# The MLP's squares on ScalarE, and another order of the three matmuls of a split product

## The chip, the cores and the metric

The kernel runs on one core of one Trainium2 chip. The time is the device time of one execution in microseconds. The kernel before was run three times: median 1261.39 us, from 1261.08 to 1261.54.

## The reference

A decoder trunk of two layers on 512 tokens with 1024 features, all in fp32. Layer 0 has a forgetting attention with 16 heads, layer 1 a gated short convolution; each is followed by an MLP and by a gated embedding. What the change touches is the MLP, and every product of a weight with activations:

```python
def sq_relu_mlp(h, w_up, w_down):
    return jnp.square(jax.nn.relu(h @ w_up)) @ w_down

for i in range(DEPTH):                       # DEPTH = 2
    ...                                      # attention (i = 0) or convolution (i = 1)
    f = sq_relu_mlp(rmsnorm(x, g[2]), w_mlp_up[i], w_mlp_down[i])
    x = x + rmsnorm(f, g[3])
    gate = jax.nn.sigmoid(rmsnorm(x, g[4]) @ w_ple_gate[i])
    e = (p[i] @ w_ple_proj[i]) * gate
    x = x + rmsnorm(e, g[5])
```

`w_mlp_up` is 1024 x 4096, `w_mlp_down` 4096 x 1024.

## The kernel before

**Split products.** A fp32 operand is kept as a pair: a high part rounded to the matmul's format (fp32r) and the low part that is left. `split` (line 230) makes it: ScalarE casts the high part, another engine subtracts it from the source for the low part (VectorE for plain weights and activations, GpSimd for weights that were combined first). `mm3` (line 222) multiplies two pairs by three matmuls into one bank of PSUM: high by high (line 224), and the two products of a low part with a high part (lines 225 and 226). Its first argument is the stationary operand, its second the moving one. There are two kinds of callers. Where `narrow` gives the weights, they are the first argument: up in the MLP, q and k, the convolution's input. Where `wide` gives them, they are the second argument and the activations the first: down in the MLP, v, the outputs of the mixers, the gated embedding. The program has 1784 such products. Names in the profile: `wh`, `wl` are a weight's parts, `hTh`, `hTl` those of the normalised and transposed tokens, `raw` a weight as loaded.

**The MLP** (`mlp`, line 704) goes over 8 groups of 512 hidden features. In a group, `up` (line 710) makes four blocks of 128 hidden features for all 512 tokens, 8 products each over the 1024 inputs (24 matmuls; in group 0 the tokens are taken in two halves of 256). ScalarE reads the bank with a relu into `r` (line 722), and `square` (line 707) makes `q = r * r`. For groups 0 to 6 `down` (line 750) multiplies by 7 products in place of 8 (a Strassen scheme over halves of the hidden features, tokens and outputs): `quarters` and `halves` make sums of quarters of `q` on GpSimd (`s`) and split them (`A11`, `A12`, `A22`, `S1` to `S4`, with h and l for the parts; the pair A12, A22 is one tile named A12, S1 and S2 one named S1, S3 and S4 one named S3); the combined weights `T1` to `T4` are made on GpSimd too. A group's `down` is 28 products, 84 matmuls of 512 columns. Its 14 banks are copied into `acc` by ScalarE in group 0 (line 765) and added to it by VectorE in the others (line 768). In group 7 there is no such scheme: ScalarE makes the high part `hh` as a rounded square of `r` (line 798), `square` the exact square, VectorE the low part `hl` as the difference (line 801), and `dn` multiplies them block by block of tokens.

**What sets the order.** Each engine runs its own queue in order. The queue's order is made when the program is built, by a scheduler that runs a model of the chip over the recorded work; only the beginning and a piece of the attention are in the order of the code. So a changed instruction can move others. PSUM's 8 banks go round: a bank is taken again when its last reader is done. Weights are loaded by SyncE's queue and split up to 8 weights ahead of their use (`SOON`, 4 or 1 in places).

Of the kernel before, what the change touches and what calls it, by code (L numbers as in the profile page):

```python
# [10 lines left out]
AF = mybir.ActivationFunctionType  # L11
ALU = mybir.AluOpType
# [52 lines left out]
def trunk(ctx: ExitStack, tc, g4T, x, pT, g, wv, wqk, bf, wo, wci, cw, wco, wup, wdn, wpp, wpg, out):  # L65
    nc = tc.nc
# [147 lines left out]
    def due():  # L214
        while later and later[0][0] <= streamed[0]:
            later.pop(0)[2]()
# [5 lines left out]
    def mm3(ps, a, b, start, stop):  # L222

        nc.tensor.matmul(ps, a.hi, b.hi, start=start, stop=False)  # L224
        nc.tensor.matmul(ps, a.lo, b.hi, start=False, stop=False)  # L225
        nc.tensor.matmul(ps, a.hi, b.lo, start=False, stop=stop)  # L226
        streamed[0] += 3 * ps.shape[-1]
        due()

# [104 lines left out]
    def mixer_out(kind, lhs, xs, gB, then, opened):  # L334


        mgs, sums = {}, {}
        for t, n in BLOCKS:
            if (t, n) == (2, 0):
                prepare(where[kind, 1, KT - 1] + 1 + SOON)  # L340
            at = (t, n) in opened
            ps = opened.pop((t, n)) if at else bank(f"{kind}{n}_{t}")
            for k in range(KT - 1 if at else 0, KT):
                mm3(ps, lhs(k, t), wide(kind, n, k, soon=soon(t, n)), k == 0, k == KT - 1)
            sums[t, n] = squares(ps, f"{kind}s{n}_{t}")
            mgs[t, n] = gained(ps, gB, n, f"{kind}m{n}_{t}")
            if (t, 1 - n) in mgs:
                residual(t, *([d.pop((t, i)) for i in range(2)] for d in (mgs, sums)), xs[t],
                         f"{kind}r")
                then(t)  # L350

    def attention(hT, first_x, g0, by_hand):
# [49 lines left out]
        def values(c, t, soon=SOON, between=None):  # L402

            c0, width = V_CHUNKS[c]
            n_v = min(width, D - c0)
            ps = bank(f"v{c}_{t}")
            for k in range(KT):
                if width == 256:
                    w = wide("v", c, k // 2).at(lambda u: u[:, k % 2 * 256 : k % 2 * 256 + 256])
                else:  # L410
                    w = wide("v", c, k, soon=soon)
                if k == 5 and between:
                    between()
                mm3(ps[:, :width], tokens(hT, k, t), w, k == 0, k == KT - 1)

            def keep_v():
                if n_v < width:
                    nc.vector.tensor_tensor(
                        out=logit[:, t * H : (t + 1) * H], in0=ps[:, n_v:width], in1=b_f,
                        op=ALU.add,  # L420
                    )
                for c1 in range(0, n_v, 256):
                    src = ps[:, c1 : c1 + 256].rearrange("p (i e d) -> p i e d", e=2, d=HD)
                    block = vs[t][(c0 + c1) // 256].rearrange("p (i r) -> p i r", i=2)
                    for e in range(2):
                        hi = block[:, :, 192 * e : 192 * e + HD]
                        lo = block[:, :, 64 + 64 * e : 128 + 64 * e]
                        split(hi, lo, src[:, :, e, :])

            return keep_v  # L430
# [3 lines left out]
        def project(i):  # L434

            q, key = (Pair(page(f"{n}h{i}", F32R), page(f"{n}l{i}", F32R)) for n in "qk")
            stacked[i] = q, key
            for s in (1, 0):
                ps = bank(f"qk{i}_{s}")
                for k in range(KT):  # L440
                    mm3(
                        ps, narrow("qk", i, k=k, c=s * P),
                        hT.at(lambda h: h[:, k, :]), k == 0, k == KT - 1,
                    )
                    if k < KT - 1:
                        yield
                if s == 0:
                    nc.scalar.mul(q.hi[:, :S], ps, HD**-0.5)
                    nc.vector.scalar_tensor_tensor(
                        out=q.lo[:, :S], in0=ps, scalar=HD**-0.5, in1=q.hi[:, :S].bitcast(F32),  # L450
                        op0=ALU.mult, op1=ALU.subtract,
                    )
                else:
                    split(key.hi[:, :S], key.lo[:, :S], ps)
                yield
# [248 lines left out]
    def mlp(l, hT, xs, then, late):  # L704
        acc = {}

        def square(out, r):
            nc.vector.tensor_tensor(out=out, in0=r, in1=r, op=ALU.mult)  # L708

        def up(gr, done, soon=lambda f: SOON):  # L710
            for lo, hi in ((0, 256), (256, 512)) if gr == 0 else ((0, 512),):
# [69 lines left out]
        for gr in range(7):  # L781
            A, s, q = {}, {}, {f: page(f"q{l}_{gr}_{f}") for f in range(4)}

            def done(f, lo, hi, r):
                square(q[f][:, lo:hi], r[:, : hi - lo])
                if lo == 0 and f % 2 == 0:
                    halves(gr, f, ("A11",), q[f], A)
                if hi == S:
                    quarters(gr, f, q, s, A)

            up(gr, done)
            down(gr, A)
# [3 lines left out]
        def done(f, lo, hi, r):  # L796
            h = Pair(*(page(f"h{s}{l}_{f}", F32R) for s in "hl"))
            nc.scalar.activation(h.hi[:, :S], r[:, :S], AF.Square)
            sq = page(f"q{l}_{f}")
            square(sq[:, :S], r[:, :S])  # L800
            nc.vector.tensor_tensor(
                out=h.lo[:, :S], in0=sq[:, :S], in1=h.hi[:, :S].bitcast(F32), op=ALU.subtract
            )
            hs.append(h)
            if f == LATE:
                gB.extend(late())

        up(7, done, lambda f: SOON + 2 * f)
        for t in range(NB):
# [6 lines left out]
            for n in range(2):  # L816
                a = total[t, n][:, :S]
# [167 lines left out]
```

## Time and profile before

| | |
|---|---|
| median of 3 runs | 1261.39 us |
| the profiled execution | 1261.29 us, span 1259.6 us |
| TensorE, matmuls | 1237.6 us busy, 98%, 6036 instructions |
| TensorE, weight loads | 1021.4 us, 81%, 6036 |
| VectorE | 897.9 us, 71%, 1370 |
| ScalarE | 608.5 us, 48%, 1293 |
| GpSimd | 628.7 us, 50%, 631 |
| clock granted to TensorE | full, 0.998 over the span |

PE stands for TensorE's matmuls, PEld for its weight loads, DVE for VectorE, ACT for ScalarE, POOL for GpSimd, SP for SyncE; a trailing q is an engine's sequencer. A row of the timeline gives the start and the length in microseconds, the engine, the line, the operation, the output and inputs by the program's names, and the size; in brackets the idle time of the engine before it and what ended it. Rows that follow each other and are alike are joined, with their count. The end of a matmul is modelled, so that matmuls overlap in the rows (0.39 us each, one begun every 0.227 us): their starts are measured. A few per cent of the matmuls' records are missing. In the list of waits a row says who waited for whom, the sum, the number of times and the longest, in microseconds.

### The profile page before, as it was taken

How to read it: one execution, taken by the hardware profiler on the slowest of the kernel's cores; microseconds unless marked ns; L12 is line 12 of the kernel's file. 1: busy time of each engine (PE TensorE's matmuls, PEld its weight loads, DVE VectorE, ACT ScalarE, POOL GpSimd, SP SyncE). 2: the span in 40 equal slices, each digit the busy share in tenths (PEclk: the TensorE clock that was granted, in tenths of full speed). 3: DMA queues.
4: the chain of work that ended last, by engine and by line, in shares of the span. 5: the costliest groups of instructions: out<-in, count | busy, mean ns of one | idle time of the engine just before them, and what ended most of it. 6: DMA issues, size and time to landing. Idle time of an engine off the chain costs nothing.

```text
span 1259.6 us, 17972 instructions
## 1 busy us (share of the span) xinstructions
PE 1237.6 (98%) x6036; PEld 1021.4 (81%) x6036; DVE 897.9 (71%) x1370; ACT 608.5 (48%) x1293; POOL 628.7 (50%) x631
## 2 busy tenths in 40 slices
PE   7999999999999999999999999999999999999997
PEld 6877777788888888887889988889788888888786
DVE  5645666767788789879967444457778897779962
ACT  5445656654645434554555333244653445535541
POOL 2017555328687777876311000016777777877310
PEclk9999999999999999999999999999999999999999
DMA  7444342262432244227613233432223442245401
GB/s 254 150 140 150 102 126 76 59 226 68 134 88 90 91 134 134 82 66 236 204 34 92 76 101 101 138 130 85 93 71 105 134 126 84 69 125 168 150 18 50
DMA packets 82939, 143.43 MB, mean 114 GB/s; under 512 B 9824, under 2 KB 17040, under 8 KB 82848
## 3 DMA queue, kind: packets, MB, share of 16 engines
q1 hardware_dynamic: 82640, 142.03, 36.2%
q8 instruction: 47, 0.77, 0.3%
q14 instruction: 44, 0.36, 0.1%
q10 hardware_dynamic: 144, 0.26, 0.1%
q0 software_dynamic: 64, 0.00, 0.0%
HBM read 135.89 MB, written 6.37 MB: 113 GB/s over the span
## 4 chain that ended last, share of the span: by engine, by line
PE 81%; DVE 8%; POOL 3%; issue 3%; ACT 2%; DMA 2%; SPq 1%; DVEq 0%; POOLq 0%; ACTq 0%
PE dn L225 6%; PE up L226 6%; PE up L224 6%; PE up L225 6%; PE dn L226 6%; PE dn L224 6%; DVE wl L233 4%; PE qk L224 3%; PE qk L226 2%; PE qk L225 2%; PE sc L484 2%; PE pg L224 2%; PE pg L226 2%; PE pg L225 2%; POOL s L736 1%
## 5 line engine op out<-in xcount | busy, mean ns | idle before, releaser
L233 DVE TENSOR_TENSOR wl<-raw,wh 128x512 fp32r<-128x512 f32 (+1 forms) x372 | 345.7, 979 | 26.2 <-ACT wh L232 25.8
L225 PE MATMUL up<-hTh,wl 128*128 128x512 f32 (+1 forms) x576 | 210.2, 365 | 0.0
L226 PE MATMUL up<-hTl,wh 128*128 128x512 f32 (+1 forms) x576 | 209.7, 366 | 0.0
L224 PE MATMUL up<-hTh,wh 128*128 128x512 f32 (+1 forms) x576 | 209.4, 366 | 0.0
L232 ACT CAST wh<-raw 128x512 fp32r<-128x512 f32 (+1 forms) x372 | 201.8, 619 | 0.1
L233 POOL TENSOR_TENSOR wl<-T,wh 128x512 fp32r<-128x512 f32 x112 | 160.8, 1468 | 35.7 <-ACT wh L232 33.2
L225 PEld LDWEIGHTS up<-hTh,wl 128*128 128x128 f32 x576 | 108.6, 189 | 17.7
L224 PEld LDWEIGHTS up<-hTh,wh 128*128 128x128 f32 x576 | 108.6, 189 | 17.4
L226 PEld LDWEIGHTS up<-hTl,wh 128*128 128x128 f32 x576 | 108.3, 189 | 17.5
L768 DVE TENSOR_TENSOR acc<-dn,acc 128x512 f32<-128x512 f32 x168 | 107.5, 679 | 10.2 <-PE dn L226 10.2
L133 POOL TENSOR_TENSOR T<-raw,raw 128x512 f32<-128x512 f32 x56 | 88.1, 1585 | 37.1 <-DMA raw<-in_wdn 28.1
L722 ACT ACTIVATE r<-up 128x512 f32<-128x512 f32 (+1 forms) x72 | 38.8, 547 | 125.9 <-PE up L226 108.1
L133 POOL TENSOR_TENSOR T<-raw,T 128x512 f32<-128x512 f32 x56 | 91.8, 1639 | 2.2
L708 DVE TENSOR_TENSOR q<-r 128x512 f32<-128x512 f32 (+1 forms) x72 | 67.9, 950 | 28.7 <-ACT r L722 28.6
L247 POOL TENSOR_SCALAR cor_r_v<-cos,cos 128x1 f32<-128x1 f32 x4 | 1.6, 397 | 159.1 <-ACT junk L255 159.1
L232 ACT CAST wh<-T 128x512 fp32r<-128x512 f32 x112 | 61.2, 617 | 0.0
L232 ACT CAST A11h<-q 128x256 fp32r<-128x256 f32 x28 | 11.4, 407 | 99.9 <-DVE q L708 99.9
L224 PE MATMUL qk<-hTh,wh 128*128 128x512 f32 x128 | 52.9, 414 | 0.0
L775 POOL TENSOR_TENSOR acc<-acc,acc 128x512 f32<-128x512 f32 x28 | 46.6, 1696 | 10.4 <-DVE acc L768 10.4
L226 PE MATMUL qk<-hTl,wh 128*128 128x512 f32 x128 | 50.7, 396 | 0.0
L225 PE MATMUL qk<-hTh,wl 128*128 128x512 f32 x128 | 50.5, 395 | 0.0
L224 PE MATMUL pg<-wh,hTh 128*128 128x512 f32 x128 | 50.3, 393 | 0.0
(240 smaller groups left out, 3097.3 us busy)
## 6 DMA issues: line engine op xcount, KB each, us to landing
raw<-in_wup SPq DMA_DIRECT2D x128, 256.0 KB, 2.9
raw<-in_wdn SPq DMA_DIRECT2D x128, 256.0 KB, 2.8
raw<-in_wci SPq DMA_DIRECT2D x48, 256.0 KB, 3.5
raw<-in_wqk SPq DMA_DIRECT2D x32, 256.0 KB, 3.3
raw<-in_wpg SPq DMA_DIRECT2D x32, 256.0 KB, 3.7
g<-in_g SPq DMA_DIRECT2D x18, 256.0 KB, 6.1
prl<-neg_c SPq DMA_DIRECT2D x16, 256.0 KB, 6.7
raw<-in_wo SPq DMA_DIRECT2D x16, 256.0 KB, 2.7
```

The lines of the kernel that those rows point to most:

```text
L133: nc.gpsimd.tensor_tensor(out=B[name, p], in0=B[a, p], in1=B[b, p], op=ALU.subtract)
L224: nc.tensor.matmul(ps, a.hi, b.hi, start=start, stop=False)
L225: nc.tensor.matmul(ps, a.lo, b.hi, start=False, stop=False)
L226: nc.tensor.matmul(ps, a.hi, b.lo, start=False, stop=stop)
L232: nc.scalar.copy(hi, src)
L233: eng.tensor_tensor(out=lo, in0=src, in1=hi.bitcast(F32), op=ALU.subtract)
L484: nc.tensor.matmul(ps[:, :nm], at[r, b * P : n], to[r, :nm], start=s == 0, stop=s == 2)
L708: nc.vector.tensor_tensor(out=out, in0=r, in1=r, op=ALU.mult)
L722: nc.scalar.activation(r[:, :n], ps[:, :n], AF.Relu)
L736: sums = lambda out, a, b, op: nc.gpsimd.tensor_tensor(out=out, in0=a, in1=b, op=op)
L768: nc.vector.tensor_tensor(out=a, in0=banks[s], in1=a, op=ALU.add)
L775: nc.gpsimd.tensor_tensor(out=a, in0=a, in1=acc[i, s][:, :S], op=ALU.add)
```

## The change

The square of groups 0 to 7 is made by ScalarE with the function Square in place of a product on VectorE, from the same `r`. In `mm3` the second and the third matmul change places. Nothing is added or left out otherwise.

```diff
     def mm3(ps, a, b, start, stop):
 
         nc.tensor.matmul(ps, a.hi, b.hi, start=start, stop=False)
-        nc.tensor.matmul(ps, a.lo, b.hi, start=False, stop=False)
-        nc.tensor.matmul(ps, a.hi, b.lo, start=False, stop=stop)
+        nc.tensor.matmul(ps, a.hi, b.lo, start=False, stop=False)
+        nc.tensor.matmul(ps, a.lo, b.hi, start=False, stop=stop)
...
         def square(out, r):
-            nc.vector.tensor_tensor(out=out, in0=r, in1=r, op=ALU.mult)
+            nc.scalar.activation(out, r, AF.Square)
```

How the queues move is seen at three places. ScalarE, layer 0, group 0, second half of the tokens (r is the relu, q the square, numbers behind a name are layer, group, block and first token):

```order
 L722 ACTIVATE r0_0_3_0_3887<-up0_0_3_0_3862 128x256
+L708 ACTIVATE q0_0_3_3677<-r0_0_3_0_3887 128x256
 L722 ACTIVATE r0_0_0_256_3915<-up0_0_0_256_3890 128x256
+L708 ACTIVATE q0_0_0_3674<-r0_0_0_256_3915 128x256
 L722 ACTIVATE r0_0_1_256_3945<-up0_0_1_256_3920 128x256
+L708 ACTIVATE q0_0_1_3675<-r0_0_1_256_3945 128x256
 L232 CAST A12h0_0_1_3948<-q0_0_1_3675 128x512
 L232 CAST S1h0_0_1_3956<-s120_0_1_3952 128x512
 L232 CAST S3h0_0_1_3960<-s340_0_0_3918 128x512
 L722 ACTIVATE r0_0_2_256_3989<-up0_0_2_256_3964 128x256
+L708 ACTIVATE q0_0_2_3676<-r0_0_2_256_3989 128x256
```

Each square stands right behind its relu, and the casts keep their places around them. VectorE, layer 0, group 7 (hl is the low part of the squares, wl a weight's):

```order
 L233 TENSOR_TENSOR wl240_6860<-raw198_6861,wh240_6859 128x512
 L233 TENSOR_TENSOR wl241_6872<-raw199_6873,wh241_6871 128x512
-L708 TENSOR_TENSOR q0_2_6888<-r0_7_2_0_6883 128x512
 L801 TENSOR_TENSOR hl0_2_6886<-q0_2_6888,hh0_2_6885 128x512
 L233 TENSOR_TENSOR wl242_6905<-raw200_6906,wh242_6904 128x512
 L233 TENSOR_TENSOR wl243_6917<-raw201_6918,wh243_6916 128x512
-L708 TENSOR_TENSOR q0_3_6933<-r0_7_3_0_6928 128x512
 L801 TENSOR_TENSOR hl0_3_6931<-q0_3_6933,hh0_3_6930 128x512
```

The squares go, and the rest of VectorE's queue stands as it stood. TensorE, layer 0, group 0, the first products with A12 (dn is a bank of `down`; L224 to L226 are the three matmuls), in the change:

```order
L224 MATMUL dn0_0_20_4064<-wh78_3731,A12h0_0_1_3948 128x512
L225 MATMUL dn0_0_20_4064<-wl78_3732,A12h0_0_1_3948 128x512
L224 MATMUL dn0_0_21_4065<-wh78_3731,A12h0_0_1_3948 128x512
L225 MATMUL dn0_0_21_4065<-wl78_3732,A12h0_0_1_3948 128x512
L224 MATMUL dn0_0_40_4090<-wh80_3787,A12h0_0_1_3948 128x512
L225 MATMUL dn0_0_40_4090<-wl80_3788,A12h0_0_1_3948 128x512
L224 MATMUL dn0_0_41_4091<-wh80_3787,A12h0_0_1_3948 128x512
L225 MATMUL dn0_0_41_4091<-wl80_3788,A12h0_0_1_3948 128x512
L226 MATMUL dn0_0_20_4064<-wh78_3731,A12l0_0_1_3949 128x512
```

Before, the same four banks had their L224 first, and the first matmul with A12l was the fifth of these rows in place of the ninth. In the narrow products the same edit works on the other operands; a product of up in group 1, before (-) and in the change (+):

```order
 L224 MATMUL up0_1_2_0_4366<-hTh_83,wh94_4178 128x512
-L225 MATMUL up0_1_2_0_4366<-hTh_83,wl94_4179 128x512
-L226 MATMUL up0_1_2_0_4366<-hTl_84,wh94_4178 128x512
+L225 MATMUL up0_1_2_0_4366<-hTl_84,wh94_4178 128x512
+L226 MATMUL up0_1_2_0_4366<-hTh_83,wl94_4179 128x512
```

Here the weights' low part `wl` comes third now, and the activations' low part second.

## The prediction

> **What bounds the kernel now.** I read the page's totals first, then TensorE's waits, then TensorE's timeline at the stage borders, and at last the timelines of ScalarE, VectorE and GpSimd where TensorE loses time.
>
> ```profile
> span 1259.6 us, 17972 instructions
> PE 1237.6 (98%) x6036; PEld 1021.4 (81%) x6036; DVE 897.9 (71%) x1370; ACT 608.5 (48%) x1293; POOL 628.7 (50%) x631
> PE dn L225 <- DVE hl L801: 2.6, 2, 1.3
> PE dn L225 <- DVE A12l L233: 0.5, 2, 0.3
> ```
>
> TensorE is busy 98% of the span, and only its lost time can be won: an engine beside it may get faster for nothing. The list of its waits names few, but a modelled end (0.39 us) hides part of each gap. So I measure from start to start. The rows below are TensorE's timeline (start, duration, line, output<-inputs). The first two are the first down matmul of group 3 and the first up matmul behind it, 84 matmuls later. Then stand the same two for group 0, for group 1 (80 matmuls between them, by the program's order) and for group 0 of layer 1; at the end the waiting matmul of group 7 in both layers.
>
> ```profile
> 429.84 0.39 PE L224 MATMUL dn<-wh,A11h 128*128 128x512 f32 x1
> 448.88 0.39 PE L224 MATMUL up<-hTh,wh 128*128 128x512 f32 x1
> ...
> 303.94 0.28 PE L224 MATMUL up<-hTh,wh 128*128 128x256 f32 x1
> 304.30 0.40 PE L224 MATMUL dn<-wh,A11h 128*128 128x512 f32 x1
> 325.68 0.39 PE L224 MATMUL up<-hTh,wh 128*128 128x512 f32 x1
> 347.44 0.39 PE L224 MATMUL dn<-wh,A11h 128*128 128x512 f32 x1
> 366.38 0.39 PE L224 MATMUL up<-hTh,wh 128*128 128x512 f32 x1
> 881.24 0.40 PE L224 MATMUL dn<-wh,A11h 128*128 128x512 f32 x1
> 902.63 0.39 PE L224 MATMUL up<-hTh,wh 128*128 128x512 f32 x1
> ...
> 595.76 0.84 PE L224 MATMUL dn<-wh,hh 128*128 128x512 f32 x3
> 597.94 0.50 PE L225 MATMUL dn<-wh,hl 128*128 128x512 f32 x1 [1.33 <-DVE hl L801]
> 598.27 0.40 PE L226 MATMUL dn<-wl,hh 128*128 128x512 f32 x1
> ...
> 1174.82 0.50 PE L225 MATMUL dn<-wh,hl 128*128 128x512 f32 x1 [1.23 <-DVE hl L801]
> ```
>
> Group 3 takes 19.04 us for 84 matmuls, 0.2267 each: an undisturbed stage. Group 0 takes 21.38 for the same 84, so 2.34 are lost; in layer 1 it is 21.39, 2.35 lost. Group 1 takes 18.94 for 80, where 18.14 are due: 0.80 lost, and I take as much for layer 1. In group 7 three matmuls from 595.76 should end their turns at 596.44, and the next starts at 597.94: 1.50 lost, in layer 1 about 0.1 less by the wait in brackets, 1.40. Together 2.34 + 2.35 + 1.60 + 2.90 = 9.2 us. That is what the change can win in the MLPs; the other groups run at the rate of group 3.
>
> **Who is late there.** Group 0 of layer 0, ScalarE, VectorE and GpSimd in turn:
>
> ```profile
> 292.67 0.38 ACT L722 ACTIVATE r<-up 128x256 f32<-128x256 f32 x1
> 298.93 0.41 ACT L232 CAST A11h<-q 128x256 fp32r<-128x256 f32 x1 [5.88 <-DVE q L708]
> 299.52 2.17 ACT L232 CAST wh<-T 128x512 fp32r<-128x512 f32 x4
> 303.38 0.93 ACT L722 ACTIVATE r<-up 128x256 f32<-128x256 f32 x3
> 306.61 0.62 ACT L232 CAST A12h<-q 128x512 fp32r<-128x512 f32 x1 [2.30 <-DVE q L708]
> 309.04 0.62 ACT L232 CAST S1h<-s 128x512 fp32r<-128x512 f32 x1 [1.81 <-POOL s L736]
> ...
> 291.61 5.86 DVE L233 TENSOR_TENSOR wl<-raw,wh 128x512 fp32r<-128x512 f32 x4
> 297.38 1.51 DVE L708 TENSOR_TENSOR q<-r 128x256 f32<-128x256 f32 x1
> ...
> 295.18 3.44 POOL L133 TENSOR_TENSOR T<-raw,T 128x512 f32<-128x512 f32 x2
> 300.21 5.41 POOL L233 TENSOR_TENSOR wl<-T,wh 128x512 fp32r<-128x512 f32 x4 [1.59 <-ACT wh L232]
> 306.38 0.80 POOL L736 TENSOR_TENSOR s<-q 128x256 f32<-128x256 f32 x1 [0.77 <-DVE q L708]
> ```
>
> ScalarE reads the relu at 292.67, and its next cast needs the square, which stands on VectorE behind four weight splits until 297.38. ScalarE's queue is held 5.88 us by that, and all it does later (the weight casts, three relus in a row at 303.38 without any wait for TensorE) comes late.
>
> **The squares.** 72 move. These rows price them: VectorE's square, and on ScalarE a Square of 512 columns and a cast of 256.
>
> ```profile
> L708 DVE TENSOR_TENSOR q<-r x72: 409/681/1782, 297.4 to 1175.9; 128x512 f32<-128x512 f32 x56, 128x256 f32<-128x256 f32 x16
> L798 ACT ACTIVATE hh<-r 128x512 fp32r<-128x512 f32 x8 | 5.1, 632 | 0.3
> L232 ACT CAST A11h<-q x28: 405/407/408, 298.9 to 1127.8; 128x256 fp32r<-128x256 f32 x28
> ```
>
> ScalarE gains 56 x 0.632 + 16 x 0.407 = 41.9 us, 650 in all of 1260; VectorE loses at least 72 x 0.409 = 29, at most 72 x 1.782 = 128. No table load is added, since Square already runs there. Neither engine is the bound, so these sums themselves count nothing; what counts is the stages.
>
> Group 0, in the new order. Relu at 292.67, square and A11h right behind (0.41 each): ScalarE is free at 293.9 instead of 299.3. Its next hold is the casts of T, which GpSimd ends at 295.18 + 3.44 = 298.62. Four casts (2.17) to 300.8; then four relus, four squares and one A11h at 0.4 each, 3.6, to 304.4: A12h is there at 305.0. TensorE wants it twelve matmuls behind 304.30, at 307.0. Covered. GpSimd's four splits start about 1 us earlier and end by 304.6; its sums begin there, not at 306.38, so S1h starts near 307.3 instead of 309.04, and is wanted 24 matmuls in, at 309.7. Covered. S3h is one sum later and ends near 308.7; behind it come two relus and two squares, and the second A12h ends near 311.0, wanted 30 matmuls in, at 311.1: the tightest point. If it slips by 0.5 us per layer, 1.0 of the 9.2 stays.
>
> Group 7 (ScalarE's relu, then VectorE) and group 1 (VectorE):
>
> ```profile
> 587.80 0.60 ACT L722 ACTIVATE r<-up 128x512 f32<-128x512 f32 x1 [1.00 <-PE up L226]
> ...
> 588.30 1.78 DVE L708 TENSOR_TENSOR q<-r 128x512 f32<-128x512 f32 x1
> ...
> 591.70 4.79 DVE L233 TENSOR_TENSOR wl<-raw,wh 128x512 fp32r<-128x512 f32 x6
> 596.41 0.68 DVE L708 TENSOR_TENSOR q<-r 128x512 f32<-128x512 f32 x1
> 597.19 0.69 DVE L801 TENSOR_TENSOR hl<-q,hh 128x512 fp32r<-128x512 f32 x1
> ...
> 353.30 1.29 DVE L768 TENSOR_TENSOR acc<-dn,acc 128x512 f32<-128x512 f32 x2 [1.30 <-PE dn L226]
> 354.51 0.97 DVE L233 TENSOR_TENSOR A12l<-q,A12h 128x512 fp32r<-128x512 f32 x1
> ```
>
> In group 7 VectorE is far behind: the relu of 587.80 is squared at 596.41, behind six weight splits, and TensorE waits for the hl that ends at 597.88. Without the two squares of these rows (1.78, and 0.78 from 596.41 to 597.19) hl ends at 595.3, before TensorE's 596.4; ScalarE has that square by 590, after the relu and hh (0.60 + 0.63 + 0.63). The whole 1.5 goes, twice.
>
> In group 1 A12l stands behind two additions that wait for TensorE itself, so it stays at 354.51 to 355.48; what helps there is the matmul order.
>
> **The matmul order.** It removes and adds no instruction. In the wide products (down among them) the stationary operand is the activations: their low part now comes third. In the narrow ones (up, qk and the convolution's, where the weights are stationary) it is the weights' low part that comes third, the opposite of the words of the change. A consumer of a late low part wins at least one matmul, 0.227 us; in groups 0 and 1 the order puts A12l eight matmuls behind its first A12h instead of four, 0.9 us more. In group 1 TensorE wanted A12l 4 matmuls in, near 354.9, and got it after 355.48; now it is wanted near 355.8. That covers most of the 0.8. On the other side a wide product needs its weights' low part one to three matmuls earlier, at worst 0.7 us at one place per group where it is the late one. No row of TensorE's waits names wl, so I take 0, and 0.7 x 16 = 11 us as the far bound, which I hold very unlikely.
>
> The first two matmuls of a product now share their stationary operand. Nearest row: in the attention two matmuls with the same v.
>
> ```profile
> 126.76 0.19 PEld L526 LDWEIGHTS ps_o<-pl,v 128*128 128x128 f32 x1
> 126.99 0.40 PE L526 MATMUL ps_o<-pl,v 128*128 128x512 f32 x1
> ```
>
> The load is issued anyway and starts 0.23 us before its matmul, as elsewhere. I take 0. Bounds: 256 columns take (304.30 - 303.94)/3 = 0.12, so 512 columns alone take about 2 x (0.2267 - 0.12) = 0.213 and the pair's overhead is 0.013; over 1784 products a skipped load would win 24 us. An uncovered one, at the 0.10 us by which 598.27 - 597.94 exceeds 0.2267 behind the wait, would lose 184.
>
> [...] The square costs VectorE from 0.41 to 1.78 us. [...]
>
> **Sum.** 1261.3 (the profiled execution's own time, 0.1 under the median) - 9.2 + 1.0 for the tight place = 1253.1; against the median 1253.2.
>
> **Rivals.** 1: half. GpSimd's sums, not the squares, set group 0 (row 309.04 waits for s); then only the low parts and group 7 win, 2.9 + 1.6 + about 1.0: 1256. For it: S1h's wait; against it: s itself waits for q at 306.38. 2: slower. ScalarE's queue becomes the late one in group 0: the eight added squares there (8 x 0.41 = 3.3 us) come on top of the old stall in both layers, no win elsewhere: 1261.4 + 6.6 = 1268. It decides once ScalarE reaches A12h after 307.0; by the walk above it is 2 us away. 3: no change. Freed time returns as waits for weights further on, since TensorE runs 9 us ahead: 1261. Against it: groups 2 to 6 run without loss at the same supply. 4: the repeated stationary operand matters, 1237 or 1445.
>
> **Chances.** Forecast 0.66, rival 1 0.17, rival 3 0.07, rival 2 0.06, rival 4 0.02 each way. A difference below 0.2% (2.5 us) can't be told from none. Faster 0.66 + 0.17 + 0.02 = 0.85, same 0.07, slower 0.08. The forecast alone spans 1251.5 to 1255 (nothing left, or twice the tight place). With rival 1 the range is 1251 to 1258; the far bounds stay outside with about 0.18.
>
> **What would show it.** In the profile of the change: group 0's 84 down matmuls in 19.1 us, group 1's near 18.2, no wait for hl in group 7; ScalarE's casts of A11h and A12h without a wait for q; VectorE near 820 us busy. Wrong if group 0 still takes over 20 us, if up matmuls wait for hTl, or if the spacing of 0.2267 changes.

## The result, and the profile after

| | runs | median, us | from - to |
|---|---|---|---|
| before | 4 | 1261.35 | 1261.08 - 1261.54 |
| the change | 4 | 1253.49 | 1252.58 - 1254.10 |

The ratio is 0.9937, its 95% interval 0.9921 to 0.9952: faster by 0.6%. The forecast was 1253.2. The profiled execution took 1253.84 us. Its totals and TensorE's whole list of waits:

```profile
span 1252.1 us, 18025 instructions
PE 1233.9 (99%) x6036; PEld 1023.5 (82%) x6036; DVE 839.4 (67%) x1298; ACT 651.9 (52%) x1365; POOL 631.2 (50%) x631
...
PE g L874 <- DMA row<-in_g: 6.6, 1, 6.6
PE n_p L272 <- DVE n_h L263: 3.0, 3, 1.6
PE ps_o L525 <- DVE pl L233: 0.5, 1, 0.5
```

No wait of the MLP is left in the list: those of `dn` for `hl` (2.6 us) and for `A12l` (0.5) are gone. The wait for `n_h`, the normalised rows at the program's start, has grown from 2.3 to 3.0. VectorE gave up 58.5 us, ScalarE took 43.4.

Where the time went is read from starts. TensorE's timeline of the change: the first down matmul of group 0 and the first up matmul behind it; the first down matmuls of groups 1 and 2; a first up matmul late in group 7 and the first transposes behind that group; then the same of layer 1, without the first pair.

```profile
305.76 0.40 PE L224 MATMUL dn<-wh,A11h 128*128 128x512 f32 x1
324.83 0.39 PE L224 MATMUL up<-hTh,wh 128*128 128x512 f32 x1
346.59 0.39 PE L224 MATMUL dn<-wh,A11h 128*128 128x512 f32 x1
387.70 0.39 PE L224 MATMUL dn<-wh,A11h 128*128 128x512 f32 x1
586.26 0.39 PE L224 MATMUL up<-hTh,wh 128*128 128x512 f32 x1
612.78 0.38 PE L272 MATMUL n_p<-ident,xd 128*128 128x128 f32 x2
...
919.08 0.39 PE L224 MATMUL dn<-wh,A11h 128*128 128x512 f32 x1
960.15 0.39 PE L224 MATMUL dn<-wh,A11h 128*128 128x512 f32 x1
1158.71 0.39 PE L224 MATMUL up<-hTh,wh 128*128 128x512 f32 x1
1185.23 0.49 PE L272 MATMUL n_p<-ident,xd 128*128 128x128 f32 x3
```

The rows of before for the pairs that the prediction did not use:

```profile
389.04 0.39 PE L224 MATMUL dn<-wh,A11h 128*128 128x512 f32 x1
587.60 0.39 PE L224 MATMUL up<-hTh,wh 128*128 128x512 f32 x1
615.75 0.49 PE L272 MATMUL n_p<-ident,xd 128*128 128x128 f32 x3
924.39 0.39 PE L224 MATMUL dn<-wh,A11h 128*128 128x512 f32 x1
966.03 0.39 PE L224 MATMUL dn<-wh,A11h 128*128 128x512 f32 x1
1164.59 0.39 PE L224 MATMUL up<-hTh,wh 128*128 128x512 f32 x1
1192.64 0.49 PE L272 MATMUL n_p<-ident,xd 128*128 128x128 f32 x3
```

Subtracting row from row, in microseconds (group 0 of layer 1 in the change goes from 878.25 to 897.32):

| stretch | before | change | difference | said in the prediction |
|---|---|---|---|---|
| start to group 0's down | 304.30 | 305.76 | +1.46 | 0 |
| layer 0, group 0, down | 21.38 | 19.07 | -2.31 | -2.34, less a slip of up to 0.5 |
| layer 0, group 1 to group 2 | 41.60 | 41.11 | -0.49 | -0.80 |
| layer 0, group 7 | 28.15 | 26.52 | -1.63 | -1.50 |
| layer 1, group 0, down | 21.39 | 19.07 | -2.32 | -2.35, less a slip of up to 0.5 |
| layer 1, group 1 to group 2 | 41.64 | 41.07 | -0.57 | -0.80 |
| layer 1, group 7 | 28.05 | 26.52 | -1.53 | -1.40 |
| sum | | | -7.39 | -9.2 + 1.0 = -8.2 |

The span fell by 7.5. So the MLPs gave 8.85 us, and 1.46 were lost before the first MLP began, at a place where the prediction had looked at nothing. Of the 1.46, 0.25 stand already at the first transposes (10.30 us, 10.05 before): the small transfer that TensorE waits for at the very start arrived at 6.63 us in place of 6.37. About 1.2 us are left for what follows.

**The start.** The views by windows of before and of the change (the first number behind the window is its length, then busy time of PE, PEld, DVE, ACT and POOL, the granted clock of TensorE, the DMA share and GB/s):

```profile
18.00:19.00 1.00, 1.00 (x11) 1.00 (x9) 1.00 (x3) 0.93 (x3) 0.00 (x0) 1.00 1.07 384
20.00:21.00 1.00, 1.00 (x10) 1.00 (x9) 0.22 (x1) 0.23 (x2) 0.59 (x2) 1.00 1.07 377
```

```profile
18.00:19.00 1.00, 1.00 (x7) 1.00 (x7) 1.00 (x2) 0.72 (x2) 0.00 (x0) 0.56 1.06 397
19.00:20.00 1.00, 1.00 (x6) 1.00 (x6) 1.00 (x3) 0.97 (x4) 0.00 (x0) 0.50 1.08 388
20.00:21.00 1.00, 1.00 (x7) 1.00 (x6) 0.47 (x1) 0.70 (x2) 0.21 (x1) 0.50 1.08 342
21.00:22.00 1.00, 1.00 (x8) 1.00 (x7) 0.23 (x1) 0.00 (x0) 0.92 (x3) 0.73 1.07 386
```

In the change TensorE had half its clock for about 3.4 us: 0.44/0.5 = 0.88 us of the first of these slices, two whole ones, 0.27/0.5 = 0.54 of the last. PE is "busy" all the while; only its count of matmuls falls, from 10 or 11 to 6 or 7 in a microsecond. The half clock follows a gap, in TensorE's timeline of the change:

```profile
14.34 0.43 PE L226 MATMUL v<-wh,hTl 128*128 128x272 f32 x1
...
15.26 0.28 PE L226 MATMUL v<-wh,hTl 128*128 128x272 f32 x1
17.17 1.53 PE L272 MATMUL n_p<-ident,n_h 128*128 128x128 f32 x8 [1.62 <-DVE n_h L263]
18.35 0.58 PE L224 MATMUL v<-wh,hTh 128*128 128x272 f32 x1
```

The value products had just become fast (rows of 0.43 us, then 0.28), and the array then stood idle for 1.62 us for the next tokens' normalised rows (`n_h`, made by VectorE). Whether the edit causes this, or whether it comes in some executions with either order, is a question for the runs below.

### The profile page after: what moved, and what is told of

Read it like the earlier page. It is cut to its first block, busy times and chain, and to the rows that moved or that the text cites. A ratio compares the mean times of both kernels' runs of the same rounds, so it can differ in the third digit from the quotient of the medians.

```text
span 1252.1 us, 18025 instructions
## 1 busy us (share of the span) xinstructions
PE 1233.9 (99%) x6036; PEld 1023.5 (82%) x6036; DVE 839.4 (67%) x1298; ACT 651.9 (52%) x1365; POOL 631.2 (50%) x631
## 3 DMA queue, kind: packets, MB, share of 16 engines
HBM read 135.89 MB, written 6.37 MB: 114 GB/s over the span
## 4 chain that ended last, share of the span: by engine, by line
PE 95%; DVE 1%; issue 1%; ACT 1%; POOL 1%; DMA 0%; POOLq 0%; DVEq 0%; ACTq 0%
PE up L226 9%; PE up L224 9%; PE up L225 9%; PE dn L226 8%; PE dn L224 8%; PE dn L225 8%; PE qk L224 3%; PE qk L226 2%; PE qk L225 2%; PE pg L224 2%; PE pg L226 2%; PE pg L225 2%; PE sc L484 2%; PE pT L503 1%; PE v L224 1%; PE v L225 1%
## 5 line engine op out<-in xcount | busy, mean ns | idle before, releaser
L233 DVE TENSOR_TENSOR wl<-raw,wh 128x512 fp32r<-128x512 f32 (+1 forms) x372 | 343.7, 971 | 26.3 <-ACT wh L232 26.2
L224 PE MATMUL up<-hTh,wh 128*128 128x512 f32 (+1 forms) x576 | 209.3, 366 | 0.0
L226 PE MATMUL up<-hTh,wl 128*128 128x512 f32 (+1 forms) x576 | 209.3, 365 | 0.0
L233 POOL TENSOR_TENSOR wl<-T,wh 128x512 fp32r<-128x512 f32 x112 | 156.4, 1427 | 32.6 <-ACT wh L232 31.3
L226 PEld LDWEIGHTS up<-hTh,wl 128*128 128x128 f32 x576 | 108.6, 189 | 17.5
L224 PEld LDWEIGHTS up<-hTh,wh 128*128 128x128 f32 x576 | 108.3, 189 | 17.5
L133 POOL TENSOR_TENSOR T<-raw,raw 128x512 f32<-128x512 f32 x56 | 92.5, 1665 | 52.0 <-DMA raw<-in_wdn 39.3
L233 DVE TENSOR_TENSOR A12l<-q,A12h 128x512 fp32r<-128x512 f32 x28 | 25.7, 918 | 43.5 <-ACT A12h L232 43.3
L233 DVE TENSOR_TENSOR A11l<-q,A11h 128x256 fp32r<-128x256 f32 x28 | 26.7, 952 | 41.1 <-ACT A11h L232 41.1
L224 PE MATMUL qk<-hTh,wh 128*128 128x512 f32 x128 | 53.0, 414 | 0.0
L226 PE MATMUL qk<-hTh,wl 128*128 128x512 f32 x128 | 50.7, 396 | 0.0
L224 PE MATMUL pg<-wh,hTh 128*128 128x512 f32 x128 | 50.5, 394 | 0.0
```

What stands on the lines that cost most here:

```text
L133: nc.gpsimd.tensor_tensor(out=B[name, p], in0=B[a, p], in1=B[b, p], op=ALU.subtract)
L226: nc.tensor.matmul(ps, a.lo, b.hi, start=False, stop=stop)
L233: eng.tensor_tensor(out=lo, in0=src, in1=hi.bitcast(F32), op=ALU.subtract)
```

## Experiments

In all of them the loss in a stretch is its length over the undisturbed one: 19.06 for group 0's down, 40.80 from group 1's down to group 2's, 26.52 for group 7, the shortest that any of these profiles has. The eight came in two series, each with its own executions of before: the first four against 1261.23 us (15 runs, 1260.67 to 1262.25), the last four against 1261.58 (9 runs, 1261.01 to 1262.56).

### The squares alone

```diff
 # the kernel before, and only this
-            nc.vector.tensor_tensor(out=out, in0=r, in1=r, op=ALU.mult)
+            nc.scalar.activation(out, r, AF.Square)
```

> The kernel before, with the squares on ScalarE and the matmul order left as it was. My theory (the squares that stood late on VectorE cost TensorE its time in groups 0 and 7; the order helps only group 1): the 84 down matmuls of group 0 take about 19.1 us in both layers instead of 21.4, group 7 has no wait for hl, group 1 keeps its 0.8 us of loss in each layer; 1261.35 - 4.7 - 2.9 = 1253.7 us if the first 25 us run as in the kernel before. The rival 'half' (the low parts' place in the matmul order made the gain in groups 0 and 7): 1256 us or more, and group 0 over 20 us. [...]

Measured: 1255.50 us (1254.32 to 1256.29, 5 runs), ratio 0.9954 (0.9941 to 0.9966); 1.8 above what was expected. Groups 0 and 7 behave as my theory has it: 304.27 to 323.33 is 19.06, and group 7 takes 26.52 in both layers. "Half" falls: the order has no part in these. But group 1 was expected to stay as it was, and got worse. TensorE's timeline of this run, the first down matmuls of groups 1 and 2 and the wait between them:

```profile
345.10 0.39 PE L224 MATMUL dn<-wh,A11h 128*128 128x512 f32 x1
353.85 0.50 PE L225 MATMUL dn<-wh,A12l 128*128 128x512 f32 x1 [0.89 <-DVE A12l L233]
356.81 0.50 PE L225 MATMUL dn<-wh,S1l 128*128 128x512 f32 x1 [0.40 <-DVE S1l L233]
387.77 0.39 PE L224 MATMUL dn<-wh,A11h 128*128 128x512 f32 x1
```

42.67 us: 1.87 lost, where before lost 0.80 (in layer 1 1.64 in place of 0.84). The 1.07 and 0.80 us by which this is more than before are the difference to the expected time. Why stands in VectorE's and GpSimd's rows of the same run:

```profile
350.96 1.29 DVE L768 TENSOR_TENSOR acc<-dn,acc 128x512 f32<-128x512 f32 x2 [5.69 <-PE dn L226]
352.17 1.63 DVE L233 TENSOR_TENSOR A12l<-q,A12h 128x512 fp32r<-128x512 f32 x1
...
348.70 0.74 POOL L736 TENSOR_TENSOR s<-q,s 128x256 f32<-128x256 f32 x1
350.69 5.51 POOL L233 TENSOR_TENSOR wl<-T,wh 128x512 fp32r<-128x512 f32 x4 [1.25 <-ACT wh L232]
```

`A12l` is ready to be made early now (its cast ends near 347.2), but VectorE's queue has two additions ahead of it that wait for TensorE's own first product, as before. What is new is its length: 1.63 us in place of 0.97. In the kernel before, GpSimd was at the last of its sums of 256 columns for the first half of that time, since they had come late, and idle for the rest; with early squares they are done by 349.4, and GpSimd is at four splits of 512 columns beside VectorE's. `S1l` behind it takes 1.53, where the kernel before has 1.11 here. In the timelines of before and of the change, the splits and squares of 512 columns on VectorE (L233 and L708) take 0.63 to 0.69 us in all 131 rows of a single one during which GpSimd ran nothing; each longer one, up to 1.78, lies beside rows of GpSimd. So I put the 1.63 us against 0.97 down to what GpSimd runs beside it, and here the price falls on the path.

### The matmul order alone

```diff
 # the kernel before, and only this
-        nc.tensor.matmul(ps, a.lo, b.hi, start=False, stop=False)
-        nc.tensor.matmul(ps, a.hi, b.lo, start=False, stop=stop)
+        nc.tensor.matmul(ps, a.hi, b.lo, start=False, stop=False)
+        nc.tensor.matmul(ps, a.lo, b.hi, start=False, stop=stop)
```

> The kernel before, with the new matmul order and the squares left on VectorE. My theory: group 1 wins about 0.5 us in each layer, group 7 one to two matmuls (0.2 to 0.5) in each, group 0 keeps at least 1.5 of its 2.3 us of loss: together 1.5 to 3, 1258.5 to 1260 us. The rival 'half': groups 0 and 7 win most of what they win in the changed kernel, 1256 us or less. [...]

Measured: 1261.43 us (1260.04 to 1262.04, 11 runs), ratio 0.9999 (0.9990 to 1.0007): nothing, and less than expected. By stretches (profiled execution, 1260.19 us): group 0 21.50, so 0.12 worse than before; group 1 40.80 in both layers, all of its loss gone; group 7 28.24 and 28.33, 0.1 and 0.3 worse. The rival that this order makes the gains of groups 0 and 7 falls again; the one or two matmuls that I gave it in group 7 are wrong too. TensorE's timeline shows why:

```profile
595.05 0.39 PE L224 MATMUL dn<-wh,hh 128*128 128x512 f32 x1
595.27 0.39 PE L225 MATMUL dn<-wl,hh 128*128 128x512 f32 x1
595.50 0.39 PE L224 MATMUL dn<-wh,hh 128*128 128x512 f32 x1
597.27 0.50 PE L226 MATMUL dn<-wh,hl 128*128 128x512 f32 x1 [1.38 <-DVE hl L801]
```

The first matmul with the late `hl` is the fourth, as it was before: the scheduler laid the other matmuls differently around it. In group 1 it is the scheduler too that helps: in VectorE's queue of this kernel `A12l` (352.61 us) stands ahead of the two additions (353.69), where before it stood behind them.

In the profiled execution the start is that of before, and the span is 1.2 us shorter. Yet the median does not show that; of the eleven executions four had a mean clock of 0.997 and took 1261.68 us on average, the other seven 1260.78. That goes to the question of the start, and does not settle all of the spread.

### The change once more

No edit.

> The changed kernel once more, for the spread of its executions. [...]

Measured: 1253.32 us; 1252.35, 1252.69, 1253.32, 1253.66, 1253.71; ratio 0.9936 (0.9923 to 0.9948). The two slowest have a mean clock of 0.997, the others 0.998 or 0.999, about 0.9 us apart, though not in two clean groups. The profiled execution (1253.66) is one of the slower two, and has the half clock again, earlier:

```profile
15.50:17.00 1.50, 0.10 (x1) 0.10 (x2) 0.91 (x2) 0.99 (x4) 0.86 (x2) 0.94 1.05 406
...
18.00:19.00 1.00, 1.00 (x7) 1.00 (x6) 1.00 (x3) 0.68 (x2) 0.00 (x0) 0.50 1.06 404
20.00:21.00 1.00, 1.00 (x9) 1.00 (x8) 0.21 (x1) 0.83 (x4) 0.04 (x1) 0.89 1.08 368
```

Its group 0 begins 0.96 us later than in the kernel before. So both profiles of this kernel have the half clock, at another moment in each; the clocks of the other executions suggest that it comes in some of them only. In group 1 this profile loses 0.31 us in layer 0 and 0.59 in layer 1, where the first one lost 0.31 and 0.27.

### TensorE kept busy through the gap

```diff
         def turn_rows(t, hs):
+            if t == 1:
+                idle = bank("idle")
+                for _ in range(6):
+                    nc.tensor.matmul(
+                        idle[:, :272], hT.hi[:, 0, :P], ready["v", 0, 0].hi, start=True, stop=True
+                    )
```

> The changed kernel, with six added matmuls of 272 columns (their result is not read) where TensorE waits for the normalized rows of the second token block, 15.5 to 17.2 us. If the idle TensorE there loses its clock: granted clock 1.00 from 18 to 21 us in every execution, and the median 0.5 to 1.1 us under that of the repeated changed kernel, near 1252.5 us. If the wait itself is all that is lost: the same time as the repeated kernel or up to 0.5 us more.

Measured: 1252.34 us (1252.18 to 1252.97, 5 runs), ratio 0.9930 (0.9917 to 0.9944); every execution has a mean clock of 0.998, and the profile a granted clock of 1.00 from 17 to 21 us. Six matmuls that nobody reads win 1 us in the median over the same kernel without them. The gap is not closed by them (1.20 us are left in the profile); it is enough that it is shorter. In group 1 this kernel's profile loses a little more than the change's, 0.61 and 0.57 us.

### Squares on ScalarE in groups 0 and 7 alone

```diff
 # the changed kernel, and
-        def square(out, r):
-            nc.scalar.activation(out, r, AF.Square)
+        def square(out, r, gr):
+            if gr in (0, 7):
+                nc.scalar.activation(out, r, AF.Square)
+            else:
+                nc.vector.tensor_tensor(out=out, in0=r, in1=r, op=ALU.mult)
```

> The changed kernel with the squares on ScalarE in groups 0 and 7 alone; in groups 1 to 6 they are on VectorE again. My theory (only the squares of groups 0 and 7 pay; in group 1 the squares on ScalarE let GpSimd's weight splits start earlier and slow VectorE's late A12l): groups 0 and 7 win 2.3 and 1.5 to 1.6 per layer as in the changed kernel, groups 2 to 6 lose nothing, group 1 wins 0.8 per layer instead of 0.5: about 0.6 us under the repeated changed kernel's median of 1253.3, 1252.3 to 1253.0. The rival (all squares pay, by the load they take from VectorE): 1253.8 us or more.

Measured: 1252.23 us (1251.78 to 1252.91, 5 runs), ratio 0.9925 (0.9911 to 0.9938). TensorE's timeline, from group 1 to group 2 in layer 0:

```profile
345.82 0.39 PE L224 MATMUL dn<-wh,A11h 128*128 128x512 f32 x1
386.62 0.39 PE L224 MATMUL dn<-wh,A11h 128*128 128x512 f32 x1
```

40.80, and in layer 1 (918.01 to 958.81) the same: no loss in group 1, and groups 2 to 6 have none either. So 48 of the 72 moved squares bring nothing, and those of group 1 cost 0.3 us per layer by the change's profile (up to 0.6 by the repeated one's). The rival that every square pays falls. The reason given for group 1 is not isolated by this run: VectorE's queue has changed too, `A12l` (350.58 us, 1.16 long) stands ahead of the two additions (351.91), as with the matmul order alone, and no longer behind them. (The profiled execution of this run had the half clock at the start; its group 0 begins 0.7 us late.)

### The old order in the first value products

```diff
 # the changed kernel, with mm3 taking a flag for the old order, and
-                mm3(ps[:, :width], tokens(hT, k, t), w, k == 0, k == KT - 1)
+                mm3(ps[:, :width], tokens(hT, k, t), w, k == 0, k == KT - 1, c == 0)
```

> The changed kernel with the old matmul order in the first four value products alone (the 96 matmuls of 272 columns in the first 25 us). [...]

Measured: 1252.43 us (1251.82 to 1252.86, 5 runs), ratio 0.9926 (0.9914 to 0.9939). The profile has the full clock from 17 to 21 us and group 0 begins at 304.30 us, as in the kernel before; no execution has a mean clock under 0.998. That is what a cause in the order would give, and five executions are few. Over all executions whose clock is on record: with the new order at the start (the change twice, the order alone, the two runs beside this one) 12 of 30 have 0.997 or less; with the old order there (before, the squares alone, this one) 5 of 34; with the six added matmuls 0 of 9. By chance alone a difference as large as that between the first two would come about 1 time in 45; but the count was made after the runs, and rests on clocks that are rounded to a thousandth (in the next run one execution at 0.996 took 1252.72 us and one at 0.999 took 1252.70). So the half clock is not the new order's alone; that this order makes it more frequent is likely, not shown. How it would do so was not isolated either: in the profile of the change the first three value matmuls take 1.12 us until the fourth begins, in that of before 1.34; in the former the rows of the value matmuls also became short earlier (0.28 us from 14.77 us on, where before still has 0.43 at 15.67; the view gives a granted clock of 1.00 for both there), TensorE was done earlier, and so waited longer for the next rows. What all ten profiles do show is the wait: where it was 0.19 to 1.53 us long (seven profiles, with the old order 0.81 in all three, with the new one 1.25 and 1.53, with the six matmuls 1.20 and 0.19) the clock stayed full; where it was 1.62, 1.88 (squares in groups 0 and 7) and 2.07 (the change again) it was halved.

### The new order in the wide products alone

```diff
 # the changed kernel, with mm3 taking a flag for the old order; set for up, q and k, and the convolution
-                        hT.at(lambda h: h[:, k, :]), k == 0, k == KT - 1,
+                        hT.at(lambda h: h[:, k, :]), k == 0, k == KT - 1, True,
```

> The changed kernel with the new matmul order in the wide products alone; in the narrow ones (up, q and k, convolution) the old order stands. My theory: the narrow order does nothing, so the time is that of the changed kernel, 1253.3 within 0.6. The rival (the narrow order matters, since the up products wait for hT's low part): 0.7 us or more away from it, with a wait of up or qk for hTl in the list.

Measured: 1252.70 us (1252.45 to 1253.52, 5 runs), ratio 0.9929 (0.9917 to 0.9942). It stands at the edge of what my theory allowed, 0.6 below 1253.3; against the kernel before of the same series its interval covers the change's 0.9936. No wait of up, q and k or the convolution for hT's low part is in the list, in this run as in all others. From group 1 to 2 its profile has the loss of the change (`A12l` 1.40 us long, a wait of 0.3). So what the order does, it does in the wide products; a gain of the old order in the narrow ones, under 1 us, is not excluded.

### The version that beats both

```diff
 # the changed kernel with the six added matmuls, and
-        def halves(gr, f, names, src, A):
+        def halves(gr, f, names, src, A, eng=nc.vector):
...
-            split(part.hi[:, :w], part.lo[:, :w], src[:, :w])
+            split(part.hi[:, :w], part.lo[:, :w], src[:, :w], eng)
...
-            halves(gr, f, ("A12", "A22"), right, A)
+            halves(gr, f, ("A12", "A22"), right, A, nc.gpsimd if gr == 1 else nc.vector)
```

> The changed kernel with the six added matmuls that keep TensorE busy at 15.5 to 17.2 us, and with group 1's low part of A12 and A22 split on GpSimd instead of VectorE. My theory: the start as in the run with the six matmuls alone (1252.34), and group 1 without its last loss of about 0.3 us per layer: 1251.8 us, at most 1252.2. The rival (GpSimd's sums, pushed back by 1 to 1.4 us, make S1 late): 1252.8 us or more, with a wait for S1h or S1l in group 1.

Measured: 1251.76 us (1251.72 to 1251.79, 4 runs), ratio 0.9921 (0.9908 to 0.9935): the fastest of all, and the steadiest. GpSimd and VectorE in group 1:

```profile
348.19 1.28 POOL L233 TENSOR_TENSOR A12l<-q,A12h 128x512 fp32r<-128x512 f32 x1
...
351.18 1.29 DVE L774 TENSOR_TENSOR acc<-dn,acc 128x512 f32<-128x512 f32 x2 [4.80 <-PE dn L226]
```

`A12l` no longer stands behind the additions and is done by 349.47; from group 1 to 2 it takes 40.80 in both layers. The sums that were pushed back by it end before they are wanted.

## Why the prediction was right, point by point

**Bound and measure.** Right. The stretches without loss kept their pace, 19.07 us for the 84 matmuls of group 0 (0.227 each). So the repeated stationary operand, which had the farthest bounds in the sum (-24 and +184), is worth nothing on this trace.

**Group 0.** Right in mechanism and size, by the squares alone. ScalarE's timeline of the change:

```profile
294.13 0.38 ACT L722 ACTIVATE r<-up 128x256 f32<-128x256 f32 x1
294.55 0.42 ACT L708 ACTIVATE q<-r 128x256 f32<-128x256 f32 x1
295.00 0.41 ACT L232 CAST A11h<-q 128x256 fp32r<-128x256 f32 x1
...
305.17 0.62 ACT L232 CAST A12h<-q 128x512 fp32r<-128x512 f32 x1
...
311.10 0.62 ACT L232 CAST A12h<-q 128x512 fp32r<-128x512 f32 x1
```

The 5.88 us hold is gone. All of it is 1.46 us later than in the walk, as TensorE is. The tightest place was mis-sized: the second `A12h` ends at 311.72 and TensorE takes it at 312.59, so 0.87 us are spare where the walk had 0.1. The allowance of 1.0 us was not needed.

**Group 7.** Right: no wait for `hl`, 26.52 in both layers, 0.13 more than the two terms of the sum in each.

**Group 1.** The sum's weakest step. "It stays at 354.51 to 355.48" took `A12l`'s place in time and its length as fixed. Counted from the first down matmul of the group, it began 0.23 us later (7.30 in place of 7.07) and ended 0.69 later, since it also got longer. VectorE in the change:

```profile
352.69 1.29 DVE L768 TENSOR_TENSOR acc<-dn,acc 128x512 f32<-128x512 f32 x2 [5.88 <-PE dn L226]
353.89 1.43 DVE L233 TENSOR_TENSOR A12l<-q,A12h 128x512 fp32r<-128x512 f32 x1
```

1.43 in place of 0.97. With 0.97 it would have ended at 354.86, and TensorE had room for it until 355.20, eight matmuls behind 353.39. In the profiles with the new order and `A12l` behind the additions, the loss follows this length: 0.06 us at 1.13, 0.27 to 0.31 at 1.38 to 1.43, 0.57 to 0.61 at 1.70 and 1.72. The order's help (1.56 of the 1.87 that the squares alone lose, and 1.37 of 1.64 in layer 1) came as I said; but the squares put their own cost there first, and 0.31 and 0.27 stayed. The reading of the 0.80 was off too. TensorE's timeline of before, in group 1 of layer 0:

```profile
355.54 0.50 PE L225 MATMUL dn<-wh,A12l 128*128 128x512 f32 x1 [0.23 <-DVE A12l L233]
...
358.08 0.50 PE L225 MATMUL dn<-wh,S1l 128*128 128x512 f32 x1
```

Four matmuls behind the first of these four banks (354.24) is 355.15, not the 354.9 of the walk, and from start to start `A12l` cost 0.49 us with the matmul behind it; 0.26 more were lost at `S1l`, which the walk did not look at.

**The start.** Not in the sum at all. I took everything ahead of the first MLP as unchanged, since no edit reached it but a swap of two matmuls; the profiled execution lost 1.46 us there, 1.2 of them with the half clock.

**The sum.** 8.2 us forecast, 8.85 won in the MLPs, 1.46 lost at the start. That the forecast time lies 0.3 from the median is due in part to two errors of opposite sign: an allowance of 1.0 that nothing used, and a loss at the start that nothing had foreseen.

**The engines' totals.** ScalarE 651.9 against 650; VectorE 839.4 against "near 820", inside its bounds of 29 to 128 us: it fell by 58.5, so 0.81 for each of the 72 squares where 820 supposes 1.08. ScalarE has four table loads (ACT_TABLE_LOAD) of 1.28 us in both profiles, so none was added.

**The rivals.** Half: fell with the first run (group 0 whole without the order). A late ScalarE: fell, no wait for it in the list. No change: fell.

## What to carry to other kernels

Move work off an engine where something waits for it, not wherever it is: here 24 of the 72 squares made all that the squares won, and those of group 1 made an early GpSimd meet a late VectorE. When an operation is made earlier, ask what it releases and beside which operation that will then run; here a length from the trace changed with what ran beside it (`A12l` in group 1: 0.97 us before, 1.63 with the squares alone). And when a gain in one place doesn't reach the total, compare starts from the first matmul on: the loss can lie where nothing was edited.

## What the runs showed of the hardware

A gap of 1.62 us in TensorE's work, some 5 us after its first transposes, was followed by half its clock for 3.4 us; the second profile of the change has it for 3.4 us again (1.5 x 0.06/0.5 = 0.18 us before 17.00, three slices of 1 us, 0.11/0.5 = 0.22 of the next), after a gap of 2.07, and so has the profile with the squares in groups 0 and 7 (1.5 x 0.04/0.5 = 0.12, three slices, 0.15/0.5 = 0.30), after one of 1.88. Value matmuls of 272 columns then start every 0.23 us in place of 0.125. It cost 1.0 to 1.2 us in the three profiles that have it (group 0 begins 1.46, 0.96 and 0.69 us later than before, the first transposes 0.25 later, 0.02 and 0.41 earlier); 12 of the 30 executions with the new order at the start have a mean clock that fits it. A gap of 1.53 us, in the profile of the new order in the wide products alone, was not followed by it. What sets the clock, and why for 3.4 us, no run isolates.
